# Gate and up projections of a SwiGLU layer: tokens as the stationary operand in six of nine chunks

## The chip, the core and the metric

The program runs on one core of a Trainium2 chip. TensorE (PE in the profile) multiplies matrices, VectorE (DVE) and ScalarE (ACT) work on the operands and results, GpSimd (POOL) and SyncE (SP) mainly issue transfers; 16 DMA engines move the data. The metric is the device time of one execution in microseconds (us). Three executions of the kernel before took 858.71, 859.27 and 859.91 us.

## The reference

One layer with three token mixers and a SwiGLU feed-forward part, for 512 tokens of 1024 channels. Only the feed-forward part is touched by the change:

```python
h2 = rms_norm(x, norm_ffn[l])
act = jax.nn.silu(jnp.einsum('bsd,df->bsf', h2, w_ffn_gate[l])) * jnp.einsum('bsd,df->bsf', h2, w_ffn_up[l])
x = x + jnp.einsum('bsf,fd->bsd', act, w_ffn_down[l])
```

The inner width is 2816. All of it is float32.

## The kernel before

**Precision.** Every float32 operand of a product is split into a high part (rounded by ScalarE with a copy) and a low part (VectorE subtracts the high part from the operand). A product is three matmuls: high by high, high by low, low by high. For a weight tile of 128 partitions by 1024 elements that is one copy on ScalarE (`split_a`, L1508, tiles `wh`) and one subtraction on VectorE (L1509, tiles `wl`). Both tiles come from a pool with three buffers each, so the split of the fourth product ahead starts when the oldest of three is used up.

**Seven products.** The inner width is cut into 11 chunks of 256 columns. Chunks 0 and 1 are computed directly (`direct_act`, with `ps_fg` and `ps_fu`). Chunks 2 to 10 are computed by a seven-product scheme for 2x2 blocks: the two halves of the 1024 input channels, the two halves of the tokens (256 each), and the two halves of the columns. The products go by the names in `ORDER`: 11, 12, S2, S1, S3, S4, 22. Four of them (S1 to S4) need sums of weight blocks, four need differences of token blocks (T1 to T4). The token blocks are prepared once (`prepare_b`): VectorE makes `hn` and the differences, ScalarE and VectorE split them into the `B0..h` and `B0..l` tiles.

**One chunk before** (`seven`, called for chunks 2 to 10). Four weight blocks (11, 21, 22, 12), each with gate and up, come by two transfers of 256 KB each (`load_a`, L1486, queue of SyncE), into the eight buffers of the pool `cor`; the load for a chunk is issued while the chunk before it is computed. VectorE makes the four sums of a chunk (`sums_a`, L1493). Each product is 24 matmuls (`product`, L315): the weights stand (128 x 128), and the 256 columns of half of the tokens move. A chunk's results lie in two PSUM tiles, `ps_y` and `ps_x`. Since S2, S3 and 22 add onto what lies in `ps_y`, ScalarE copies parts of it out in between (`tx` and `ty`, L1562): the matmuls of S3 may not begin before the copy behind S2 has been made. `finish_act` adds the last parts, applies Silu and multiplies.

**What sets the order.** A scheduler arranges each engine's instructions once, when the program is built; on the chip each engine works through its own list in order and stands still at an instruction whose operands are missing. The transfers wait in the lists of the engine that issues them (SP or POOL) in the same way. `make_a` is called three products ahead.

**Other weights in this kernel** are already used with tokens standing and 512 weight columns moving: the q, k and v projections (`tok_product`, L844, tiles `ps_q`). There some sums of blocks are made by transfers that add onto what lies in SBUF (`accum_op`, only issued by GpSimd), and the results are turned in 32 x 32 blocks by VectorE (L814).

Of the kernel before, what the change touches and what calls it, by code (L numbers as in the profile page):

```python
# [27 lines left out]
WARM = 9  # L28
GBUFS = 27
NDIRECT = 2  # L30
KD = 10
NTICK = (1, 1)
H = S // 2
# [29 lines left out]

@with_exitstack
def layer_kernel(ctx: ExitStack, tc: tile.TileContext, x, xt, vecs, w_in, w_qkv7, w_gate7, w_pool, w_rg, w_ig,
                 w_branch, w_br7, w_out, w_fg, w_fu, w_fd, w_fd7, out):
    nc = tc.nc
    act = nc.scalar.activation
    dve = nc.vector
# [21 lines left out]
    def cols(ap, k0, nk, c0, nc_):  # L91
        return ap[k0 * P:(k0 + nk) * P, c0:c0 + nc_].rearrange("(k p) c -> p k c", p=P)
# [878 lines left out]
    with ExitStack() as mix:  # L971
# [299 lines left out]
        def corner(shape, name, dt=F32):  # L1271

            return cor.tile([P] + shape, dt, tag="r", name=name)
# [91 lines left out]
    with ExitStack() as ffn:  # L1365
# [85 lines left out]
            dve.tensor_tensor(l, BN[key], h.bitcast(F32), ALU.subtract)  # L1451
            B[which, nm] = h, l

        def diff_b(nm, x, y):
            BN[nm] = corner([4, H], f"hn{nm}")
            dve.tensor_tensor(BN[nm], BN[x], BN[y], ALU.subtract)

        def prepare_b():
            nrm = [lambda k=k: norm2(k) for k in range(8)]
            return nrm[:4] + [lambda: split_b("11", (0, 0))] + nrm[4:] + [  # L1460
                lambda: split_b("21", (1, 0)),
                lambda: diff_b("T1", (0, 1), (0, 0)),
                lambda: diff_b("T2", (1, 1), "T1"),
                lambda: split_b("T2", "T2"),
                lambda: split_b("T1", "T1"),
                lambda: diff_b("T3", (1, 1), (0, 1)),
                lambda: split_b("T3", "T3"),
                lambda: split_b("22", (1, 1)),
                lambda: diff_b("T4", (1, 0), "T2"),
                lambda: split_b("T4", "T4")]  # L1470

        SUMS = {"S2": (("S3", "11", "21", ALU.subtract), ("S2", "22", "S3", ALU.subtract)),
                "S1": (("S1", "21", "22", ALU.add),),
                "S4": (("S4", "12", "S2", ALU.subtract),)}

        DOWN = NF // 2
        steps = [(c, nm) for c in range(NDIRECT, DOWN) for nm in ORDER]
        raw = {}
        A = {}
        made = [0, NDIRECT]  # L1480

        def load_a(c):
            for nm in ("11", "21", "22", "12"):
                raw[c, nm] = t = corner([2, 4, P], f"w{c}_{nm}")
                for w in range(2):
                    nc.sync.dma_start(t[:, w], cols((w_fg, w_fu)[w], KH[nm] * 4, 4, c * 256 + CH[nm] * P, P))  # L1486

        def sums_a(c, nm):
            for s_, x, y, op in SUMS.get(nm, ()):
                if (c, s_) in raw:  # L1490
                    continue
                raw[c, s_] = t = wp.tile([P, 2, 4, P], F32, tag="raw", name=f"w{c}_{s_}")
                dve.tensor_tensor(t, raw[c, x], raw[c, y], op)  # L1493

        def make_a(upto):
            while made[0] < min(upto, len(steps)):
                c, nm = steps[made[0]]
                made[0] += 1
                while made[1] < min(c + 2, DOWN):
                    load_a(made[1])  # L1500
                    made[1] += 1
                sums_a(c, nm)
                A[c, nm] = split_a(raw[c, nm], f"{c}_{nm}")

        def split_a(src, n):
            h, l = (t.rearrange("p (w k c) -> p w k c", w=2, k=4)
                    for t in weight_tiles("wh" + n, "wl" + n))
            act(h, src, AF.Copy)  # L1508
            dve.tensor_tensor(l, src, h.bitcast(F32), ALU.subtract)  # L1509
            return h, l  # L1510

        acts = []
        DB = {}


# [17 lines left out]
        def finish_act(t, ps, a):  # L1533

            v = two2(t)
            dve.tensor_tensor(v, v, in_order2(ps), ALU.add)
            act(t[:, 0, :], t[:, 0, :], AF.Silu)
            dve.tensor_tensor(a, t[:, 0, :], t[:, 1, :], ALU.mult)


        PRE = ("S2", "S1", "S3")
# [1 line left out]
        def seven(c):  # L1543
            a = g4([2, S], f"act{c}")
            tx, ty = g4([2, S], f"tx{c}"), g4([2, S], f"ty{c}")
            Y = fp.tile([P, 2, S], F32, tag="mm", name=f"ps_y{c}")
            X = fp.tile([P, 2, S], F32, tag="mm", name=f"ps_x{c}")
            lo, hi = slice(0, H), slice(H, S)
            plan = (("11", Y, 1, True, tx, lo, Y, hi),
                    ("12", X, 0, True, None, None, None, None),  # L1550
                    ("S2", Y, 1, False, tx, hi, Y, hi),
                    ("S1", X, 1, False, ty, hi, X, hi),
                    ("S3", Y, 1, False, ty, lo, Y, hi),
                    ("S4", X, 1, False, None, None, None, None),
                    ("22", Y, 0, False, None, None, None, None))
            n0 = steps.index((c, "11"))
            for n, (nm, ps, half, first, t, ts_, src, ss) in enumerate(plan):
                with tc.issue_after(last) if (c, n) == (NDIRECT, 3) else nullcontext():
                    make_a(n0 + n + 3)
                product(A.pop((c, nm)), B[0, WITH[nm]], ps, half, first, True)  # L1560
                if t is not None:
                    last = act(two2(t[:, :, ts_]), in_order2(src[:, :, ss]), AF.Copy).ins  # L1562
                if c == DOWN - 1 and nm in PRE:
                    split_d2("11", PRE.index(nm), 0, 0)
                if nm == "S4":
                    finish_act(tx, X, a[:, 0, :])
                if nm == "22":
                    finish_act(ty, Y, a[:, 1, :])
                if (c, n) in after:
                    after[c, n]()  # L1570
            acts.append(a)

        bg.extend([lambda: None, rms2] + prepare_b())
        for c in range(NDIRECT):
# [12 lines left out]

            if c < NDIRECT - 1:
                direct_act(0), direct_act(1)
            acts.append(a)  # L1590
        tick(len(bg))
        after = {(NDIRECT, 1): lambda: direct_act(0), (NDIRECT, 2): lambda: direct_act(1)}
# [164 lines left out]


_INS = ["x", "xt", "vecs", "w_in", "w_qkv7", "w_gate7", "w_pool", "w_rg", "w_ig", "w_branch", "w_br7", "w_out",
        "w_ffn_gate", "w_ffn_up", "w_ffn_down", "w_down7"]  # L1760


# [41 lines left out]
```

## Time and profile before

| what | value |
|---|---|
| median of three executions | 859.27 us |
| the profiled execution | 858.89 us |
| its span in the profile | 856.8 us |
| TensorE busy | 850.3 us (99%) |
| VectorE busy | 732.3 us (85%) |
| ScalarE busy | 533.3 us (62%) |
| GpSimd busy | 88.6 us (10%) |
| mean transfer rate | 180 GB/s |

In the profile a matmul's duration includes the time in which its results drain, while the next one already runs; the time that it takes away from the others is the distance from one start to the next. TensorE's clock was granted in full all through. Times inside the span are counted from its start. The gate and up products of chunks 2 to 10 lie at 580.50 to 749.46 us, behind the two direct chunks and ahead of the down projection.

### The profile page before, as it was taken

How to read it: one execution, taken by the hardware profiler on the slowest of the kernel's cores; microseconds unless marked ns; L12 is line 12 of the kernel's file. 1: busy time of each engine (PE TensorE's matmuls, PEld its weight loads, DVE VectorE, ACT ScalarE, POOL GpSimd, SP SyncE). 2: the span in 40 equal slices, each digit the busy share in tenths (PEclk: the TensorE clock that was granted, in tenths of full speed). 3: DMA queues.
4: the chain of work that ended last, by engine and by line, in shares of the span. 5: the costliest groups of instructions: out<-in, count | busy, mean ns of one | idle time of the engine just before them, and what ended most of it. 6: DMA issues, size and time to landing. Idle time of an engine off the chain costs nothing.

```text
span 856.8 us, 14307 instructions
## 1 busy us (share of the span) xinstructions
PE 850.3 (99%) x5483; PEld 781.2 (91%) x5483; DVE 732.3 (85%) x937; ACT 533.3 (62%) x863; POOL 88.6 (10%) x128
## 2 busy tenths in 40 slices
PE   9999999999999999999999999999999999999998
PEld 7888888888889988889889988889999999999998
DVE  7899898987897699967997877799988888999974
ACT  6554999658887657556665544455655555755642
POOL 1110002123324102000001100000000000121200
PEclk9999999999999999999999999999999999999999
DMA  9586356798585768846668854364533434797913
GB/s 343 160 286 205 101 167 200 215 316 262 141 257 129 228 170 239 246 116 171 174 204 212 182 197 148 99 164 136 145 99 109 114 101 142 221 238 204 199 32 123
DMA packets 141988, 154.09 MB, mean 180 GB/s; under 512 B 41696, under 2 KB 115424, under 8 KB 141920
## 3 DMA queue, kind: packets, MB, share of 16 engines
q1 hardware_dynamic: 129248, 107.30, 40.6%
q0 software_dynamic: 12528, 45.62, 22.5%
q8 instruction: 43, 0.70, 0.3%
q10 hardware_dynamic: 144, 0.26, 0.1%
q14 instruction: 25, 0.20, 0.1%
HBM read 132.71 MB, written 18.87 MB: 177 GB/s over the span
## 4 chain that ended last, share of the span: by engine, by line
PE 88%; ACT 4%; DVE 4%; issue 3%; POOL 1%; DMA 0%; DVEq 0%; POOLq 0%
PE ps_y L315 11%; PE ps_x L315 8%; PE ps_dy L1723 6%; PE ps_q L844 5%; PE ps_dx L1723 5%; PE ps_br L306 3%; PE ps_br L307 3%; PE ps_br L308 3%; PE ps_bY L1347 3%; PE ps_gy L315 3%; PE ps_gate L736 2%; PE ps_bX L1347 2%; PE ps_gx L315 2%; PE ps_pool L308 2%; PE ps_pool L306 2%
## 5 line engine op out<-in xcount | busy, mean ns | idle before, releaser
L141 ACT ACTIVATE whi<-raw 128x1024 fp32r<-128x1024 f32 x69 | 72.9, 1056 | 75.6 <-PE ps_br L307 18.4
L142 DVE TENSOR_TENSOR wlo<-raw,whi 128x1024 fp32r<-128x1024 f32 x69 | 84.2, 1220 | 22.4 <-ACT whi L141 21.9
L142 DVE TENSOR_TENSOR wlo<-qw,whi 128x1024 fp32r<-128x1024 f32 x48 | 58.3, 1220 | 11.6 <-ACT whi L141 11.2
L141 ACT ACTIVATE whi<-qw 128x1024 fp32r<-128x1024 f32 x48 | 50.4, 1052 | 23.6 <-PE ps_q L844 12.8
L1508 ACT ACTIVATE wh_S<-w_S 128x1024 fp32r<-128x1024 f32 x36 | 38.3, 1063 | 28.7 <-PE ps_y L315 20.0
L1629 POOL DMA_DIRECT2D dw<-in_w_down_dram x20 | 17.0, 855 | 305.3 <-DMA dw<-in_w_down_dram 247.7
L1509 DVE TENSOR_TENSOR wl_S<-w_S,wh_S 128x1024 fp32r<-128x1024 f32 x36 | 43.8, 1220 | 3.3 <-ACT wh_S L1508 3.3
L1508 ACT ACTIVATE wh<-w 128x1024 fp32r<-128x1024 f32 x27 | 28.6, 1061 | 28.0 <-PE ps_x L315 9.4
L1509 DVE TENSOR_TENSOR wl<-w,wh 128x1024 fp32r<-128x1024 f32 x27 | 32.9, 1220 | 8.2 <-ACT wh L1508 8.2
L1508 ACT ACTIVATE whdS<-dw 128x1024 fp32r<-128x1024 f32 x20 | 21.2, 1061 | 20.7 <-PE ps_dy L1723 10.6
L1155 DVE TENSOR_TENSOR_SCAN E<-K,ahead 128x512 f32<-128x512 f32 (+3 forms) x32 | 25.4, 814 | 4.6 <-ACT K L1151 4.6
L1509 DVE TENSOR_TENSOR wldS<-dw,whdS 128x1024 fp32r<-128x1024 f32 x20 | 24.3, 1221 | 5.2 <-ACT whdS L1508 5.2
L306 PE MATMUL ps_lru<-HH,whi 128*128 128x512 f32 x64 | 24.6, 384 | 0.0
L306 PE MATMUL ps_br<-yph,whi 128*128 128x512 f32 x64 | 24.4, 382 | 0.0
L306 PE MATMUL ps_gate<-HH,whi 128*128 128x512 f32 x64 | 24.4, 381 | 0.0
L307 PE MATMUL ps_br<-ypl,whi 128*128 128x512 f32 x64 | 24.3, 380 | 0.0
L306 PE MATMUL ps_pool<-HH,whi 128*128 128x512 f32 x64 | 24.3, 379 | 0.0
L306 PE MATMUL ps_br<-yHH,whi 128*128 128x512 f32 x64 | 24.3, 379 | 0.0
L307 PE MATMUL ps_lru<-HL,whi 128*128 128x512 f32 x64 | 24.3, 379 | 0.0
L308 PE MATMUL ps_lru<-HH,wlo 128*128 128x512 f32 x64 | 24.3, 379 | 0.0
L307 PE MATMUL ps_gate<-HL,whi 128*128 128x512 f32 x64 | 24.3, 379 | 0.0
L308 PE MATMUL ps_gate<-HH,wlo 128*128 128x512 f32 x64 | 24.3, 379 | 0.0
(742 smaller groups left out, 3432.1 us busy)
## 6 DMA issues: line engine op xcount, KB each, us to landing
raw<-in_w_in_dram SPq DMA_DIRECT2D x31, 512.0 KB, 5.1
qw<-in_w_qkv_dram SPq DMA_DIRECT2D x24, 512.0 KB, 7.2
dw<-in_w_down_dram POOLq DMA_DIRECT2D x20, 512.0 KB, 7.7
w<-in_w_ffn_gate_dram SPq DMA_DIRECT2D x36, 256.0 KB, 3.9
w<-in_w_ffn_up_dram SPq DMA_DIRECT2D x36, 256.0 KB, 4.1
raw<-in_w_branch_dram SPq DMA_DIRECT2D x16, 512.0 KB, 3.8
qw<-in_w_qkv_dram POOLq DMA_DIRECT2D x12, 512.0 KB, 7.6
g<-gd SPq DMA_DIRECT2D x24, 256.0 KB, 4.5
```

Source lines behind the costliest of these rows:

```text
L141: act(hi, raw, AF.Copy)
L142: los.append(dve.tensor_tensor(lo, raw, hi.bitcast(F32), ALU.subtract).ins)
L306: nc.tensor.matmul(ps, lh, rh, start=start, stop=False, skip_group_check=skip)
L307: nc.tensor.matmul(ps, lh, rl, start=False, stop=False, skip_group_check=skip)
L308: nc.tensor.matmul(ps, ll, rh, start=False, stop=stop, skip_group_check=skip)
L315: nc.tensor.matmul(o, a_[a][:, w, k, :], il2(b_[b][:, k, :]), start=first and n == k == 0, stop=last and n == 2 and k == 3, skip_group_che ...
L844: nc.tensor.matmul(ps[:, a, :], b_[:, k, ts_], il(a_[:, kk, :]), start=first and n == k == 0, stop=n == 2 and k == 3, skip_group_check=True)
L1155: dve.tensor_tensor_scan(E[:, c0:c0 + n][:, ::-1], K[:, c0 + 1:c0 + n + 1][:, ::-1], ahead[:, S - n:][:, ::-1], 0.0, ALU.mult, ALU.add)
L1347: nc.tensor.matmul(o, ah[x_][:, w, k, :], il2(b[k][y_]), start=first_ and n == k == 0, stop=n == 2 and k == 3, skip_group_check=True)
L1508: act(h, src, AF.Copy)
L1509: dve.tensor_tensor(l, src, h.bitcast(F32), ALU.subtract)
L1723: nc.tensor.matmul(o, a_[a][:, w, k0 + k, :], il2(b_[b][:, k, :]), start=first and i == k == 0, stop=last and i == 2 and k == nk - 1, skip ...
```

## The change

`NTOK = 3`. Chunks 2 to 7 become three units of two chunks (512 gate columns and 512 up columns each; `seven_tok`). In a unit the 2x2 blocks have gate against up as their column halves. Every product is now two pieces of 12 matmuls, in which a 128 x 128 block of tokens stands and 512 weight columns move. The results have the tokens on the partitions. ScalarE copies them out (`snap`), VectorE adds (`add`), ScalarE applies Silu, VectorE multiplies, turns the product in blocks of 32 x 32, and GpSimd stores it to a scratch tensor `ad` in DRAM; SyncE reads it back with the channels on the partitions (`load_act`), during the unit or chunk that follows. The order of the channels that this gives is answered by reordering the rows of the down weights on the host.

Chunks 8 to 10 keep weights standing and 256 token columns moving. What changes for them, too, is how the sums of weight blocks are made: with other signs of T1, T2 and T4 all sums become additions, and transfers issued by GpSimd make them (21+22; 11+21+22; then 21 onto 11, and 12 onto S2). In the units VectorE makes S2 (two additions a unit), transfers the others. The weights are laid out on the host so that every load is 512 KB of whole rows.

```diff
+NTOK = 3
...
-        def sums_a(c, nm):
-            for s_, x, y, op in SUMS.get(nm, ()):
...
-                dve.tensor_tensor(t, raw[c, x], raw[c, y], op)
...
+        def load_a(u):
+            if u >= NTOK:
+                for nm, more in (("11", ()), ("21", ("22",)), ("S2", ("21", "22"))):
+                    raw[u, nm, 0] = t = corner([2, 4, P], f"w{u}_{nm}")
+                    base = "11" if nm == "S2" else nm
+                    nc.sync.dma_start(t, lsrc(u, base))
+                    for m in more:
+                        nc.gpsimd.dma_start(t, lsrc(u, m), accum_op=ALU.add)
+                return
+            for nm in ("11", "21"):
+                for i in range(2):
+                    raw[u, nm, i] = t = corner([2, 512], f"w{u}_{nm}{i}")
+                    nc.sync.dma_start(t, usrc(u, nm, i))
+                    if nm == "21":
+                        nc.gpsimd.dma_start(t, usrc(u, "22", i), accum_op=ALU.add)
...
         def make_a(upto):
...
+                if u >= NTOK:
+                    for at, m in (("11", "12"), ("S1", "22")):
+                        if nm == at:
+                            raw[u, m, 0] = t = wp.tile([P, 2, 4, P], F32, tag="raw", name=f"w{u}_{m}")
+                            nc.sync.dma_start(t, lsrc(u, m))
+                    src = raw[u, FROM.get(nm, nm), 0]
+                    A[u, nm, i] = split_a(src, f"{u}_{nm}")
+                    for at, m in (("11", "21"), ("S2", "12")):
+                        if nm == at:
+                            nc.gpsimd.dma_start(src, lsrc(u, m), accum_op=ALU.add)
+                    continue
...
+                A[u, nm, i] = split_a(src, f"{u}_{nm}{i}", (2, 512))
+                if nm == "11":
+                    raw[u, "S2", i] = t = g4([2, 512], f"w{u}_S2{i}")
+                    dve.tensor_tensor(t, raw[u, "21", i], src, ALU.add)
+                    nc.gpsimd.dma_start(src, usrc(u, "21", i), accum_op=ALU.add)
+                elif nm == "S2":
+                    nc.gpsimd.dma_start(src, usrc(u, "12", i), accum_op=ALU.add)
...
+        def seven_tok(u):
...
+            def done(j):
+                g, t = v["g", j], v["u", j]
+                act(g, g, AF.Silu)
+                dve.scalar_tensor_tensor(t, t, -1.0, g, ALU.mult, ALU.mult)
+                dve.transpose(g.rearrange("p a c -> p (a c)"), t.rearrange("p a c -> p (a c)"))
+                for h in range(2):
+                    n = 4 * (2 * j + h)
+                    nc.gpsimd.dma_start(ad[u][:, n:n + 4].rearrange("m b (j i) -> (b j) m i", i=P),
+                                        g[:, h].rearrange("p (m i) -> p m i", i=P))
...
+                for i in range(2):
+                    make_a(n0 + 2 * n + i + 3)
+                    ah, al = A.pop((u, nm, i))
+                    for a in range(2):
+                        ts_ = slice(a * P, (a + 1) * P)
+                        for kk in range(2):
+                            k = 2 * i + kk
+                            for m, (b_, a_) in enumerate(((bh, ah), (bh, al), (bl, ah))):
+                                nc.tensor.matmul(ps[dst][:, a, :], b_[:, k, ts_], il(a_[:, kk, :]),
...
-        for c in range(NDIRECT, NF // 2):
-            if c == NF // 2 - 1:
+        for u in range(NTOK):
+            seven_tok(u)
+        for c in range(NDIRECT + 2 * NTOK, DOWN):
+            if c == DOWN - 1:
```

TensorE, the first matmuls of the gate and up products before. A row names the line, the operation, what is written, then what moves and what stands; `B011h` is the high part of token block 11, `wh2_11` the high part of chunk 2's weight block 11:

```order
L315 MATMUL ps_y2_5831<-B011h_5547,wh2_11_5811 128x256
L315 MATMUL ps_y2_5831<-B011l_5548,wh2_11_5811 128x256
L315 MATMUL ps_y2_5831<-B011h_5547,wl2_11_5812 128x256
L315 MATMUL ps_y2_5831<-B011h_5547,wh2_11_5811 128x256
L315 MATMUL ps_y2_5831<-B011l_5548,wh2_11_5811 128x256
```

The same place now; `wh0_110` is the high part of unit 0, block 11, piece 0, and `ps_yh0` the first result tile of the unit:

```order
L1665 MATMUL ps_yh0_5833<-wh0_110_5814,B011h_5550 128x512
L1665 MATMUL ps_yh0_5833<-wl0_110_5815,B011h_5550 128x512
L1665 MATMUL ps_yh0_5833<-wh0_110_5814,B011l_5551 128x512
L1665 MATMUL ps_yh0_5833<-wh0_110_5814,B011h_5550 128x512
L1665 MATMUL ps_yh0_5833<-wl0_110_5815,B011h_5550 128x512
```

What moves and what stands have changed places, and one matmul now does the columns of two.

VectorE at the start of the gate and up products before. `sg..` belong to the direct chunks, `w2_S3` and `w2_S2` are sums of chunk 2:

```order
L1509 TENSOR_TENSOR wl2_11_5812<-w2_11_5787,wh2_11_5811 128x1024
L1585 TENSOR_TENSOR sg00_5667<-sg00_5667,ps_fu_0_5577 128x512
L1585 TENSOR_TENSOR sg01_5672<-sg01_5672,ps_fu_0_5577 128x512
L1586 TENSOR_TENSOR act0_5666<-sg00_5667,rb2_5160 128x512
L1586 TENSOR_TENSOR act0_5666<-sg01_5672,rb2_5160 128x512
L1509 TENSOR_TENSOR wl2_12_5816<-w2_12_5796,wh2_12_5815 128x1024
L1493 TENSOR_TENSOR w2_S3_5819<-w2_11_5787,w2_21_5790 128x1024
L1583 TENSOR_TENSOR sg10_5888<-ps_fg_1_5677,rb2_5160 128x512
```

The same place now; `w0_210` is unit 0's block 21, piece 0, onto which a transfer has added block 22:

```order
L1550 TENSOR_TENSOR wl0_110_5815<-w0_110_5790,wh0_110_5814 128x1024
L1704 TENSOR_TENSOR sg00_5670<-sg00_5670,ps_fu_0_5580 128x512
L1704 TENSOR_TENSOR sg01_5675<-sg01_5675,ps_fu_0_5580 128x512
L1705 TENSOR_TENSOR act0_5669<-sg00_5670,rb2_5160 128x512
L1705 TENSOR_TENSOR act0_5669<-sg01_5675,rb2_5160 128x512
L1538 TENSOR_TENSOR w0_S20_5818<-w0_210_5794,w0_110_5790 128x1024
L1550 TENSOR_TENSOR wl0_111_5822<-w0_111_5792,wh0_111_5821 128x1024
L1538 TENSOR_TENSOR w0_S21_5825<-w0_211_5797,w0_111_5792 128x1024
L1702 TENSOR_TENSOR sg10_5900<-ps_fg_1_5680,rb2_5160 128x512
L1702 TENSOR_TENSOR sg11_5943<-ps_fg_1_5680,rb2_5160 128x512
L1550 TENSOR_TENSOR wl0_120_5829<-w0_120_5810,wh0_120_5828 128x1024
```

The two sums of S2, which need the transfers that add, stand ahead of the low parts of the second and third pieces (`wl0_111`, `wl0_120`).

ScalarE in the third of the chunks that keep their form (chunk 10, weights named `w5` now), from the split of S3 on; `tx10` is the copy out of PSUM behind S2. Before:

```order
L1508 ACTIVATE wh10_S3_7738<-w10_S3_7675 128x1024
L1508 ACTIVATE wh10_S4_7775<-w10_S4_7773 128x1024
L1562 ACTIVATE tx10_7671<-ps_y10_7673 128x2x256
L1508 ACTIVATE wh10_22_7810<-w10_22_7379 128x1024
L1562 ACTIVATE ty10_7672<-ps_x10_7674 128x2x256
```

Now:

```order
L1549 ACTIVATE wh5_S3_7188<-w5_11_6825 128x1024
L1549 ACTIVATE wh5_S4_7223<-w5_S2_6830 128x1024
L1603 ACTIVATE tx10_7124<-ps_y10_7126 128x2x256
L1549 ACTIVATE wh5_22_7258<-w5_22_7158 128x1024
L1603 ACTIVATE ty10_7125<-ps_x10_7127 128x2x256
```

The order is the same, but the split of S4 now reads `w5_S2`, onto which a transfer adds block 12 after the split of S2; before, VectorE had made that sum.

More of the change, by code (lines that the diff above doesn't have):

```diff
@@ L1510, in split_a @@
             return h, l
-        acts = []
+        acts = {}
         DB = {}
@@ L1555, in seven @@
                     ("22", Y, 0, False, None, None, None, None))
-            n0 = steps.index((c, "11"))
+            u = NTOK + c - (NDIRECT + 2 * NTOK)
+            n0 = steps.index((u, "11", 0))
             for n, (nm, ps, half, first, t, ts_, src, ss) in enumerate(plan):
-                with tc.issue_after(last) if (c, n) == (NDIRECT, 3) else nullcontext():
-                    make_a(n0 + n + 3)
-                product(A.pop((c, nm)), B[0, WITH[nm]], ps, half, first, True)
+                make_a(n0 + n + 3)
+                product(A.pop((u, nm, 0)), B[0, WITH[nm]], ps, half, first, True)
                 if t is not None:
@@ L1565, in seven @@
                 if nm == "S4":
-                    finish_act(tx, X, a[:, 0, :])
+                    finish_act(tx, X, a[:, 0, :], 1.0)
                 if nm == "22":
[L1568 to L1571, printed above, removed]
+                    finish_act(ty, Y, a[:, 1, :], -1.0)
+                if toload and nm in LOADS.get(u - NTOK, ()):
+                    with tc.issue_after(last):
+                        load_act()
@@ new lines, in seven, with load_act @@
+            acts[c] = a
+        ad = [dr.tile([4, S // 32, 4096], F32, tag=f"ad{u}", name=f"ad{u}") for u in range(NTOK)]
+        toload = []
+        LOADS = {0: ("S3",), 1: ("11",)}
+        def load_act():
+            c = toload.pop(0)
+            u, m = divmod(c - NDIRECT, 2)
+            acts[c] = t = g4([2, S], f"act{c}")
+            for w in range(2):
+                nc.sync.dma_start(t[:, w].rearrange("p (b i) -> p b i", i=32),
+                                  ad[u][2 * m + w].rearrange("b (p i) -> p b i", i=32))
```

122 lines of the change are left out of this document (89 added, 33 removed).

## The prediction

> **What bounds the kernel now.** I read the page's busy times first, then the windows of the stage, then the chain of waits through it.
>
> ```profile
> span 856.8 us, 14307 instructions
> PE 850.3 (99%) x5483; PEld 781.2 (91%) x5483; DVE 732.3 (85%) x937; ACT 533.3 (62%) x863; POOL 88.6 (10%) x128
> ```
>
> TensorE stands still for 6.5 us in all. The windows give each engine's busy time in the stage of chunks 2 to 7, then of chunks 8 to 10:
>
> ```profile
> 580.50:693.18 112.68, 112.68 (x1010) 112.64 (x1010) 103.22 (x97) 64.29 (x80) 0.00 (x0) 1.00 0.44 122
> 693.18:749.46 56.28, 56.28 (x506) 56.28 (x505) 50.03 (x49) 35.31 (x46) 2.57 (x3) 1.00 0.50 150
> ```
>
> The columns behind the length are PE, PEld, DVE, ACT, POOL, the clock, the DMA share and GB/s. TensorE never waits in either, and so a microsecond is worth a microsecond here. VectorE is at 92% of the first window, POOL does nothing, the transfers take under half. The chain names TensorE alone, with start, length and count:
>
> ```profile
> 580.50 2.68 PE ps_y L315 x24
> 583.17 2.68 PE ps_x L315 x24
> 585.85 2.70 PE ps_y L315 x24
> ...
> 728.02 5.36 PE ps_y L315 x48
> 733.38 2.68 PE ps_x L315 x24
> ...
> 741.42 2.68 PE ps_y L315 x24
> ```
>
> Each product of 24 matmuls of 256 columns takes 2.68 us, 111.7 ns each. The row of 48 holds the last product of one chunk and the first of the next, so chunk 10 begins at 730.70. A product in the new form (tokens standing, 512 weight columns moving) already runs in the q projections, where nothing makes it wait:
>
> ```profile
> 166.16 5.18 PE ps_q2S L844 x24
> ```
>
> That is 215.8 ns each, 107.9 for 256 columns.
>
> **The change part by part.** *Matmuls.* Six chunks have 42 products of 2.68 us, 112.6 us. Three units have 42 pieces of 12 matmuls, 42 x 5.18/2 = 108.8 us. Gain 3.8 us, all on the path. The bounds: nothing, if the spacing came out as before, and 3.9 with the 0.1 us that the first window has above 112.6.
> The Trainium skill (TensorE: Matmul & The Clock Gate, Back-to-back issue gap) gives N/2.4 GHz + 2.5 ns from start to start; that is 215.8 ns at 512 columns, as in the trace, but 109.2 at 256, where the trace has 111.7. By the page's formula the gain would be an estimated 1.3 us, not 3.8. The row measured in this very stage decides.
>
> *VectorE and ScalarE.* What the units issue, by these groups (count, busy us, mean ns):
>
> ```profile
> L1509 DVE TENSOR_TENSOR wl_S<-w_S,wh_S 128x1024 fp32r<-128x1024 f32 x36 | 43.8, 1220 | 3.3 <-ACT wh_S L1508 3.3
> L1493 DVE TENSOR_TENSOR w_S<-w,w 128x1024 f32<-128x1024 f32 x18 | 22.0, 1223 | 0.5
> L1493 DVE TENSOR_TENSOR w_S<-w,w_S 128x1024 f32<-128x1024 f32 x18 | 22.0, 1223 | 0.5
> L814 DVE STREAM_TRANSPOSE sq<-r 128x1024 f32<-128x1024 f32 x8 | 9.9, 1241 | 0.5 <-ACT r L823 0.5
> ```
>
> The 36 sums, four a chunk, go; a unit gets 14 low parts, 2 sums, 4 additions out of PSUM and 2 multiplications (I take 1.22 for each of the 22) and 2 turns of 1.24: 29.3 us of VectorE in 36.3 us, 81% against 92%. Followed step by step, an operand in a unit is ready at least 1.8 us before TensorE needs it, so I cost this at nothing. Its cover is TensorE's next two pieces, 5.2 us; if that were gone, the copies out of PSUM would delay the next product first. The 12 stores and 12 loads of turned results have a whole unit or chunk to land: nothing.
>
> *The start.* VectorE's two S2 sums of unit 0 wait for transfers that add 22 onto 21, and two low parts stand behind them. The load under the second sum goes into a buffer that before came free at 569.65; the groups are SP's issue, VectorE at that time, and landings of these loads:
>
> ```profile
> 569.65 0.37 SPq L1486 DMA_DIRECT2D w<-in_w_ffn_gate_dram  x1
> 578.70 1.22 DVE L1509 TENSOR_TENSOR wl<-w,wh 128x1024 fp32r<-128x1024 f32 x1
> L1486 SPq DMA_DIRECT2D w<-in_w_ffn_gate_dram x2: 368/612/857, 569.6 to 570.7; - x2
> DMA to landing us min/median/max: 4.1/4.9/5.2
> ```
>
> So POOL can issue the second addition at 574.55. What one takes is seen in other stages, behind loads and in a quieter place:
>
> ```profile
> L1282 POOL DMA_DIRECT2D bw<-in_w_br_dram x2: 848/870/892, 432.4 to 435.1; - x2
> DMA to landing us min/median/max: 8.6/8.6/8.6
> L270 POOL DMA_DIRECT2D bw<-in_w_br_dram x6: 835/844/852, 449.5 to 477.5; - x6
> DMA to landing us min/median/max: 5.1/5.6/8.8
> ```
>
> Nearest is the pair with loads beside it: 8.6, landing at 583.15. Then come the second sum (1.14 from start to start), two operations of direct chunk 1 (0.60 each) and the low part of the third piece (1.22): it is ready at 586.7. TensorE wants it two pieces after 580.50, at 585.7. Wait 1.1 us (with 5.1 none, with 8.8 1.3). The first sum, ready two microseconds earlier, is hidden by the first piece.
>
> *S4 in chunks 8 to 10.* Block 12 is added onto S2's buffer after S2's split. ScalarE's split of S4 stands ahead of the copy of `ps_y` behind S2, which S3 needs. In chunk 10 before (VectorE's split of S2, ScalarE's split of S4, the copy):
>
> ```profile
> 733.81 2.35 DVE L1509 TENSOR_TENSOR wl_S<-w_S,wh_S 128x1024 fp32r<-128x1024 f32 x2
> 738.72 1.07 ACT L1508 ACTIVATE wh_S<-w_S 128x1024 fp32r<-128x1024 f32 x1 [1.66 <-PE ps_y L315]
> 739.69 0.58 ACT L1562 ACTIVATE tx<-ps_y 128x512 f32<-128x512 f32 x1
> ```
>
> The copy ends at 740.27, S3 begins at 741.42: the split may be 1.15 us late, so the addition has to land by 739.87, 9.17 us into the chunk. The first split of the VectorE row ends at 735.0, 4.3 into the chunk, since the last addition and multiplication of chunk 9 and `al` lie ahead of it, then as now. Left over: 4.85 us. Chunk 9 begins 7 x 2.68 earlier, at 711.94; there the S2 split (the second row) ends 2.6 into the chunk, left over 6.5:
>
> ```profile
> 711.57 0.69 DVE L1538 TENSOR_TENSOR act<-tx 128x512 f32<-128x512 f32 x1
> 713.31 1.22 DVE L1509 TENSOR_TENSOR wl_S<-w_S,wh_S 128x1024 fp32r<-128x1024 f32 x1
> ```
>
> In chunk 8 the last multiplication and turn of unit 2 push the split to about 3.1, an estimate by the durations above; left over 6.0. Nearest for the additions are the first two of the down stage, at the same place in the program:
>
> ```profile
> L1629 POOL DMA_DIRECT2D dw<-in_w_down_dram x2: 849/853/857, 730.6 to 732.4; - x2
> DMA to landing us min/median/max: 5.4/5.9/6.5
> ```
>
> I take 5.9 for chunks 9 and 10, and 6.5 for chunk 8, which has two stores beside it. Waits: 0.5 + 0 + 1.1 = 1.6 us. The ends: at 5.1 it is 0.3 in chunk 10 alone, at 8.8 it is 2.8 + 2.3 + 4.0 = 9.1.
>
> *POOL's list* now has 33 additions and 12 stores ahead of or between those of the down stage. Where S2 of chunk 10 is built by two additions, the second waits for the first, and the S3 addition of chunk 9 stands behind both. It still lands some 3 us early by my walk through; likewise the one for chunk 10 behind `dw210`. Late next, if they slip: S3 of chunk 9. Cost nothing, bound 3 us.
>
> *Sum.* -3.8 + 1.1 + 1.6 = -1.1 us. From the profiled execution's 858.89 (2.1 beside its span) that is 857.8; the median of the runs lies 0.4 above that execution, so 858.2.
>
> **The rivals.** *The additions land early.* With the 5.1 to 5.6 of the quieter row everywhere nothing waits at the start nor in chunks 8 and 9, and 0.3 to 0.8 in chunk 10. For it: the DMA share of the stage is 0.44 to 0.50. Against: the start has a burst of loads. Time: -3.5 to -3.0, 855.8 to 856.3, say 856.0.
> The Trainium skill (DMA: Bandwidth & Descriptors, Anatomy of one DMA) fits a transfer issued by GpSimd as 2.0 us and its bytes at 436 GB/s, an estimated 3.2 us for 512 KB; by that nothing would wait at all and the sum would be 3.8 us less than before. No addition in this trace lands below 5.1.
>
> *The additions land late: slower.* One mechanism, the time L of one addition, decides at four places: the start (L - 7.5), chunk 8 (L - 6.0), chunk 9 (L - 6.5), chunk 10 (L - 4.85), each not below nothing. At the median of the down stage's 20,
>
> ```profile
> dw<-in_w_down_dram POOLq DMA_DIRECT2D x20, 512.0 KB, 7.7
> ```
>
> the waits are 0.2 + 1.7 + 1.2 + 2.85 = 5.95 us, 2.2 more than the gain: 861.4. From L = 7.1 on (start nothing, 3 x 7.1 - 17.35 = 3.9) it is slower than before. The landing times of 8.8 to 11.8 in a crowded part of that stage would make it worse; against it speaks that this crowd is of additions behind each other, here they are apart.
>
> *The spacing does not come down.* If TensorE gained nothing from the longer matmul, 2.7 us of waits would be added: 862. The q projections' row speaks against it; a half of the gain with my waits is 860.1, no difference.
>
> **How the numbers follow.** A measurement here tells 0.2% (1.7 us) from no change: faster means below 857.5, slower above 861.0. My case, waits of 2 to 4 us: chance 0.45, own range 857.0 to 859.8, a fifth of it faster. Early additions: 0.30, faster. Late additions: 0.17, slower. Half the spacing: 0.08, three parts no difference and one slower. Faster 0.09 + 0.30 = 0.39; no change 0.36 + 0.06 = 0.42; slower 0.19. The range from 855.4 (early additions, 0.4 to spare for the 0.1 us and the spread of the runs) to 861.8 (just past the late case's centre) leaves about 0.15 outside.
>
> **What would show it.** Right: rows of 12 or 24 matmuls with 512 columns spaced 216 ns in the units; TensorE's idle time small inside units 1 and 2; a wait of about 1 us for VectorE's third low part near 585; in chunk 10 a gap of about 1 us ahead of S3, with ScalarE's S4 split waiting for a transfer. VectorE at about 81% in the units. Wrong: gaps at unit ends or behind the copies out of PSUM, a wait for loads that SyncE issues behind `act` loads, or additions of over 8 us in chunks 8 to 10.

## The result, and the profile after

| | before | after |
|---|---|---|
| median of the executions | 859.48 us (858.71 to 859.91, 4) | 881.21 us (876.96 to 884.13, 4) |
| profiled execution / its span | 858.89 / 856.8 us | 880.38 / 878.6 us |

The ratio is 1.025, 95% interval 1.021 to 1.029: slower by 22 us, 19 us past the upper end of the predicted range. The page after, its span and its busy times:

```profile
span 878.6 us, 13277 instructions
PE 853.0 (97%) x4979; PEld 768.5 (87%) x4979; DVE 704.4 (80%) x907; ACT 530.6 (60%) x845; POOL 126.1 (14%) x173
```

TensorE now stands still for 25.6 us where it was 6.5. The windows of the units, then of chunks 8 to 10 (columns as before: length, PE, PEld, DVE, ACT, POOL, clock, DMA share, GB/s):

```profile
580.99:695.50 114.51, 111.19 (x507) 96.46 (x506) 85.26 (x76) 62.52 (x62) 26.47 (x32) 0.99 1.00 247
695.50:770.80 75.30, 60.87 (x504) 60.30 (x504) 41.81 (x41) 34.32 (x44) 12.27 (x16) 0.91 0.97 243
```

Before, these were 112.68 and 56.28 us with a DMA share of 0.44 and 0.50. Of the 21.8 us that the span grew, 20.9 lie here, 19.0 of them in three chunks whose matmuls did not change. The DMA engines are now busy nearly all through in both (shares of 1.00 and 0.97). The list of waits of TensorE shows where it stood:

```profile
PE ps_y L316 <- ACT tx L1603: 14.4, 3, 9.4
PE ps_xl L1665 <- DVE wl L1550: 2.2, 1, 2.2
PE ps_yh L1665 <- DVE wl L1550: 1.1, 1, 1.1
```

The first row is three stops of 14.4 us in all, the longest 9.4: S3 of chunks 8, 9 and 10, which waits for the copy `tx`. The other two are the start. The chain of waits (start, length, what; a DMA from its issue to its landing):

```profile
574.98 11.52 DMA w<-in_w_ffn_dram
590.13 6.92 PE ps_xl L1665 x23
679.93 5.18 PE ps_yh L1665 x24
698.85 15.04 DMA w_S<-in_w_ffnl_dram
714.96 0.59 ACT tx L1603
715.59 5.31 PE ps_y L316 x24
738.51 2.94 PE ps_y L316 x24
751.66 7.68 DMA w_S<-in_w_ffnl_dram
761.04 4.57 PE ps_y L316 x24
```

The products in the units take 5.18 us as forecast. The DMA rows are additions, the one in chunk 8 with 15 us. And behind three of the stops the same 24 matmuls take longer than without a stop: 6.92 for 5.18, 5.31 and 4.57 for 2.68, 6.3 us in all. (Behind the short stop in chunk 9 it is 2.94, at the full clock.) The windows of 2 us say why; behind the length stand PE, PEld, DVE, ACT, POOL, and then the clock:

```profile
592.00:594.00 2.00, 2.00 (x6) 1.55 (x6) 2.00 (x4) 0.48 (x1) 0.00 (x0) 0.50 1.05 223
718.00:720.00 2.00, 2.00 (x11) 2.00 (x11) 0.00 (x0) 0.00 (x0) 0.00 (x0) 0.50 1.04 203
722.00:724.00 2.00, 2.00 (x21) 2.00 (x20) 1.52 (x2) 0.86 (x2) 0.56 (x1) 1.00 1.08 168
```

TensorE is busy all through in each. But in the second window, at half the clock, it has 11 matmuls of 256 columns in hand, in the third, at the full clock, 21; of these it begins 9 and 18, the others still drain from the window before. ScalarE's rows of chunk 8 (what ended its idle time stands in brackets) show that S4 was not the only late block:

```profile
707.44 1.06 ACT L1549 ACTIVATE wh_S<-w 128x1024 fp32r<-128x1024 f32 x1 [7.83 <-DMA w<-in_w_ffnl_dram]
714.00 1.06 ACT L1549 ACTIVATE wh_S<-w_S 128x1024 fp32r<-128x1024 f32 x1 [5.50 <-DMA w_S<-in_w_ffnl_dram]
```

The first row is S3's block; TensorE had reached S3 at 706.2. The account of the stage: -3.8 for the matmuls, +17.7 in stops, +6.3 at the lower clock, 0.7 not assigned, 20.9.

### The profile page after: what moved, and what is told of

It reads as the page before. It is cut to its first block, busy times and chain, and to the rows that moved or that the text cites. A ratio compares the mean times of both kernels' runs of the same rounds, so it can differ in the third digit from the quotient of the medians.

```text
span 878.6 us, 13277 instructions
## 1 busy us (share of the span) xinstructions
PE 853.0 (97%) x4979; PEld 768.5 (87%) x4979; DVE 704.4 (80%) x907; ACT 530.6 (60%) x845; POOL 126.1 (14%) x173
## 4 chain that ended last, share of the span: by engine, by line
PE 71%; issue 9%; DVE 7%; DMA 6%; ACT 5%; POOL 2%; SPq 0%; ACTq 0%; POOLq 0%; DVEq 0%
PE ps_dy L1844 6%; PE ps_q L845 5%; PE ps_dx L1844 5%; PE ps_yh L1665 5%; PE ps_xh L1665 4%; PE ps_y L316 3%; PE ps_br L308 3%; PE ps_br L309 3%; PE ps_br L307 3%; DMA w_S<-in_w_ffnl_dram 3%; PE ps_bY L1348 2%; PE ps_gy L316 2%; DVE wlo L143 2%; PE ps_xl L1665 2%; PE ps_bX L1348 2%
## 5 line engine op out<-in xcount | busy, mean ns | idle before, releaser
L1550 DVE TENSOR_TENSOR wl_S<-w_S,wh_S 128x1024 fp32r<-128x1024 f32 x18 | 22.0, 1223 | 24.6 <-ACT wh_S L1549 24.6
L1550 DVE TENSOR_TENSOR wl_S<-w,wh_S 128x1024 fp32r<-128x1024 f32 x18 | 22.0, 1223 | 22.2 <-ACT wh_S L1549 22.2
L1549 ACT ACTIVATE wh_S<-w_S 128x1024 fp32r<-128x1024 f32 x18 | 19.0, 1053 | 21.6 <-DMA w_S<-in_w_ffnl_dram 10.0
L1549 ACT ACTIVATE wh_S<-w 128x1024 fp32r<-128x1024 f32 x18 | 19.0, 1057 | 20.6 <-DMA w<-in_w_ffnl_dram 9.7
L308 PE MATMUL ps_br<-yHL,whi 128*128 128x512 f32 x64 | 24.4, 381 | 0.1
```

The lines of the kernel that those rows point to most:

```text
L308: nc.tensor.matmul(ps, lh, rl, start=False, stop=False, skip_group_check=skip)
```

## The experiments

Times are medians, the ratio is to the kernel before on the same chip.

**VectorE's sums in chunks 8 to 10.**

```diff
-                for nm, more in (("11", ()), ("21", ("22",)), ("S2", ("21", "22"))):
+                for nm in ("11", "21", "22", "12"):
                     raw[u, nm, 0] = t = corner([2, 4, P], f"w{u}_{nm}")
+                    nc.sync.dma_start(t, lsrc(u, nm))
...
+                        dve.tensor_tensor(t, raw[u, x, 0], raw[u, y, 0], ALU.add)
```

> The kernel after, but in chunks 8 to 10 VectorE makes the four sums again from four plainly loaded blocks; the 15 additions by transfer of these chunks are gone, the units stay as they are. Theory (the S3 and S4 additions of these chunks land late and hold ScalarE and TensorE; the stops then cost clock as well): the stops of 9.4, about 1.7 and about 3.5 us and the slower matmuls behind them (2.6 and 1.9 us) go, 19 us less than after, about 861 to 862; the three chunks take 56.3 us as before. Rival 1 (the loads of act in pieces of 128 bytes crowd the queue of SyncE and the DMA engines, whatever makes the sums): the plainly loaded blocks come late as well, 868 or more, with waits for transfers in chunks 8 to 10. Rival 2 (VectorE had no room there): slower than 862 with waits for VectorE.

859.02 us, ratio 1.000 (0.999 to 1.001): 22 us less than after, 2 to 3 more than the theory asked for. The three chunks take 56.27 us without a stop:

```profile
693.38:749.65 56.27, 56.27 (x505) 56.27 (x505) 53.25 (x52) 34.50 (x45) 5.68 (x7) 1.00 0.73 205
```

The units, with all their additions, stores and loads, cost nothing beyond the start; VectorE has room at 95% (53.25 of 56.27).

**The start, too.**

```diff
+                    if nm == "21" and u == 0:
+                        t2 = wp.tile([P, 2, 512], F32, tag="raw", name=f"w{u}_e22{i}")
+                        nc.sync.dma_start(t2, usrc(u, "22", i))
+                        dve.tensor_tensor(t, t, t2, ALU.add)
```

> As the run before this one, and in unit 0 VectorE also adds block 22 onto block 21 from a plain load (1 MB more loaded, two VectorE operations of about 1.2 us). Theory (the start loses 3.4 us to two late additions and 1.8 us to the clock behind these stops): 5 us less than with the chunks' sums alone, about 856 to 857, which is a little faster than before the change. Rival (the loads at the start are late by themselves, because the transfers of the whole stage are crowded there): no or under 2 us less, 859 or more.

857.18 us, ratio 0.9969 (0.9958 to 0.998): this version is faster than both kernels. One stop of 0.4 us is left in the stage, and its two windows add up to 165.55 us where before had 168.96:

```profile
580.25:689.52 109.27, 108.88 (x506) 95.34 (x506) 86.53 (x79) 62.21 (x62) 19.08 (x24) 1.00 0.90 227
689.52:745.80 56.28, 56.28 (x505) 56.28 (x505) 53.27 (x52) 34.49 (x45) 5.79 (x8) 1.00 0.73 203
```

That is the matmuls' 3.8 us less the one stop: the first term of the prediction, seen alone. The medians of the two versions differ by 1.8 us where 5 were expected. In the trace of the other version the start has the stops of after (2.2 and 1.0 us), but the clock stays at 1.00, so in that execution the 1.8 us of clock were not there to gain (four of its ten executions have a mean clock of 0.998, and they are the four longest); of the other 3.2 us the profiled spans show 3.5, the medians less, and this version's profiled execution, 855.29 us, is its shortest.

**S4 alone by VectorE.**

```diff
+                    if nm == "S4":
+                        dve.tensor_tensor(raw[u, "S2", 0], raw[u, "S2", 0], raw[u, "12", 0], ALU.add)
...
-                    for at, m in (("11", "21"), ("S2", "12")):
+                    for at, m in (("11", "21"),):
```

> The kernel after, but in chunks 8 to 10 VectorE adds block 12 onto S2's buffer (from the plain load of 12 that is there for the product 12 anyway), so the S4 additions by transfer are gone, and nothing else: four additions a chunk are left, S3's among them. Theory (S4's addition is the longest of several late ones): S3's block in chunk 8 stays 3 us late, the stops of chunks 9 and 10 shrink to under 2 us, 864 to 870. Rival (the prediction's step alone, late S4 additions, is the whole loss): all stops of chunks 8 to 10 go, 860 to 863, as with all sums by VectorE.

872.61 us, ratio 1.016 (1.014 to 1.017): 8.6 us less than after, smaller than either side said. The additions of S4 are gone, and `ps_y` waits for `tx` all the same, 7.0 us in two stops: now for S3's addition, which lands 9.9 us behind its issue in chunk 9. So it is not S4 alone. That addition was also issued late. On GpSimd's list it stands behind the second addition to S2 of chunk 10, which waits for the landing of the first (the chain, POOL being the issues):

```profile
711.75 0.91 POOL w_S L1498
...
718.99 0.57 POOL w_S L1498
719.56 9.89 DMA w<-in_w_ffnl_dram
```

Chunk 9 begins at 716.33 here, so the issue is 3.2 us into the chunk; in the kernel after it was 2.7 us ahead of it. This is the slip that the prediction called "late next".

**The copy ahead of the split.**

```diff
+                    with tc.issue_after(cp[0]) if nm == "S4" else nullcontext():
+                        A[u, nm, i] = split_a(src, f"{u}_{nm}")
```

> The kernel after with one order changed: in chunks 8 to 10 ScalarE's split of S4 stands behind the copy tx that S3 waits for, not ahead of it. All additions stay. Theory (the DMA engines are full there and every added block comes late, S3's as well as S4's): in chunk 8 S3's own block is split only at about 708.5, 3 us late, and S4's block, landed at 713.9, comes 2 us later than S4 could begin, so most of the stop only moves from S3 to S4: 3 to 8 us less than after, 872 to 878. Rival (the place of the split ahead of the copy is the cause, as the prediction priced it): the stops of chunks 8 to 10 go, 862 to 866.

877.3 us, ratio 1.021 (1.020 to 1.023): 3.9 us less than after. The stops moved, from S3 to the product behind it:

```profile
PE ps_x L316 <- ACT ty L1605: 7.1, 2, 5.1
PE ps_y L316 <- ACT tx L1605: 2.9, 1, 2.9
```

The place of ScalarE's split adds a little; the late blocks are the loss.

**S2 by VectorE: three of ten transfers fewer, S3 and S4 untouched.**

```diff
-                for nm, more in (("11", ()), ("21", ("22",)), ("S2", ("21", "22"))):
+                for nm, more in (("11", ()), ("21", ("22",))):
...
+                    if nm == "11":
+                        raw[u, "S2", 0] = t = g4([2, 4, P], f"w{u}_S2")
+                        dve.tensor_tensor(t, raw[u, "21", 0], src, ALU.add)
```

> The kernel after, but in chunks 8 to 10 VectorE makes S2 from the buffers of 21 (with 22 added) and 11, as in the units; the load and the two additions that made S2 are gone, three of ten transfers of 512 KB a chunk. S3's and S4's additions stay by transfer, at the same places. Theory (how late S4's addition lands depends on how much else the DMA engines and GpSimd's queue carry there): they land in 7 to 9 us instead of 15.0, 7.7 and 7.7, stops of 3 to 8 us in all, 865 to 873. Rival (S4's addition is late for its own place, whatever else is carried): 877 or more, the chain still names over 12 us for it in chunk 8.

864.77 us, ratio 1.008 (1.006 to 1.009): 16.4 us less than after, though the additions that TensorE waits for kept their places. They land in 5.4 to 10.7 us, 7.0 at the median (after: 6.6 to 15.0, 8.0), and the stops for `tx` are 4.3 us. What is late depends on what else is under way. But this also took a wait out of GpSimd's list, where the second addition to S2 stands behind the landing of the first; two runs look at the two apart.

**The same transfers, another order on GpSimd.**

```diff
+                        if u == NTOK:
+                            nc.gpsimd.dma_start(t, lsrc(u, m), accum_op=ALU.add)
+                        else:
+                            later.append((t, lsrc(u, m)))
...
+                            with tc.issue_after(s4.ins):
+                                nc.gpsimd.dma_start(*later.pop(0), accum_op=ALU.add)
```

> The kernel after with all its transfers, but in another order on GpSimd's list: the additions that build 21+22 and S2 of chunks 9 and 10 stand behind the S4 addition of the chunk before, not ahead of its S3 addition. Theory A (the loss comes from GpSimd's list: an addition that waits for the one before it on the same buffer holds S3's and S4's additions behind it): S3's addition of chunk 8 is issued several us earlier, the stops of chunks 8 to 10 shrink to 2 to 6 us, 862 to 868, about what leaving S2's additions out gave (864.8). Theory B (the number of bytes on the DMA engines): the additions land as late as before, 874 to 882; the stops may move to later chunks. Between, 868 to 874, both have a part.

879.87 us, ratio 1.023 (1.022 to 1.025): no gain that the intervals can tell. Five stops instead of three, 16.8 us instead of 14.4, and in other places: 1.5 us where chunk 8 had 9.4, but 10.3 in chunk 10. There the additions for S3 and S4 stand on the list behind a transfer of the down projection that starts at 747.84, 9.6 us into the chunk:

```profile
747.84 0.84 POOL L1758 DMA_DIRECT2D dw<-in_w_down_dram  x1 [10.27 <-DVE Bd110l L1579]
748.38 1.17 POOL L1532 DMA_DIRECT2D w<-in_w_ffnl_dram  x1
748.91 1.51 POOL L1532 DMA_DIRECT2D w_S<-in_w_ffnl_dram  x1
```

So this order takes a loss away at one end of the list and makes one at the other. It doesn't show that the list has no part.

**Two loads back.**

```diff
+                for n in range(2):
+                    nc.sync.dma_start(corner([2, 4, P], f"wx{u}_{n}"), lsrc(u, ("11", "21")[n]))
```

> VectorE makes S2 of chunks 8 to 10 (864.8 before), and SyncE loads two blocks of 512 KB a chunk more into buffers that nobody reads, in the place of the load and the two additions that were left out. Theory B (bytes): most of the loss comes back, 872 to 880. Theory A (GpSimd's list): the two loads hold nobody on GpSimd, 864 to 868.

870.67 us, ratio 1.013 (1.011 to 1.016): 5.9 us come back with two plain loads of 512 KB a chunk that nobody reads and nobody on GpSimd waits for. The additions for S3 and S4 land later with them. The landing times without the two loads, then with them:

```profile
DMA to landing us min/median/max: 5.4/7.0/10.7
```

```profile
DMA to landing us min/median/max: 7.8/8.5/11.2
```

The time is a little under the 872 of the theory of bytes and outside its rival's 864 to 868. So more transfers alone make the additions late. Of the other 10.5 us it stays open how much is the higher price of an addition (measured in the next run) and how much the wait in the list.

**Chunk additions without units.** Chunks 2 to 7 as in the first run, chunks 8 to 10 as after, no stores and loads of `act`.

```diff
-NTOK = 3
+NTOK = 0
+ADD0 = 6
...
+            if u < ADD0:
+                for nm in ("11", "21", "22", "12"):
```

> No units: all nine chunks have weights standing and 256 columns moving; chunks 2 to 7 get their sums from VectorE, chunks 8 to 10 from additions by transfer exactly as after. No stores and loads of act. Theory (the additions land late since the transfers of the units, the stores and the loads of act are still going on): in the quiet stage ahead they land in 5 to 8 us as the prediction took them, the waits are 1 to 6 us, 860 to 866. Rival (ten transfers of 512 KB in 18.8 us a chunk are too many by themselves): 870 or more, with stops of over 5 us for additions in chunks 8 to 10.

869.97 us, ratio 1.012 (1.010 to 1.014), between the two: stops of 7.9 us, the longest 4.1, in a stage that was quiet ahead. So ten transfers a chunk cost 11 us by themselves; with the units ahead of them the same additions cost 22 (859.0 to 881.2). Its queues in a quiet stretch (590 to 650: 13 plain loads) and in the crowded one (690 to 755: additions on q0) tell the price of each (packets, MB, share of 16 engines):

```profile
q1 hardware_dynamic: 1872, 6.82, 33.7%
...
q0 software_dynamic: 1630, 5.96, 53.5%
q1 hardware_dynamic: 2314, 7.46, 31.0%
```

33.7% of 60 us over 13 loads is 1.55 us of all 16 engines for one of 512 KB; 53.5% of 65 us for 5.96 MB is 3.06 us for an addition of 512 KB, twice as much. The last row, of the plain loads beside these additions, gives 1.42 us for 512 KB, so it is not the crowd that makes the difference. An estimate from the first two rows, of the engines' time that a chunk of 18.76 us asks for (the loads of `act` and of the down weights left out), beside the measured length of the three chunks (from the first matmul of chunk 8 to the first of the down projection):

| version | loads + additions a chunk | engines' time a chunk (estimate) | chunks 8 to 10 |
|---|---|---|---|
| sums by VectorE | 4 + 0 | 6.2 us | 56.3 us |
| S2 by VectorE | 4 + 3 | 15.4 us | 62.9 us |
| two loads back | 6 + 3 | 18.5 us | 68.8 us |
| S4 by VectorE | 5 + 4 | 20.0 us | 66.5 us |
| after | 5 + 5 | 23.1 us | 75.5 us |

After asks for more than the chunk lasts. The only pair out of order is the version without S4's addition, which takes away a transfer that TensorE waits for. The table goes with the crowd, but the versions differ in GpSimd's list as well.

**Long pieces.** The turned results are stored and read back in pieces of 2 KB, in another order, so the channels of `act` come out of order.

```diff
-                nc.sync.dma_start(t[:, w].rearrange("p (b i) -> p b i", i=32),
-                                  ad[u][2 * m + w].rearrange("b (p i) -> p b i", i=32))
+                nc.sync.dma_start(t[:, w], ad[u][2 * m + w].rearrange("b (q c) -> (b q) c", c=512))
```

> The kernel after with all its additions, but the turned results are stored and read back in pieces of 2 KB instead of 512 and 128 bytes (the same bytes, in another order, so the channels of act come out of order). Theory A (the small pieces fill the DMA engines and delay the additions): the additions in chunks 8 to 10 land in 6 to 8 us, the stops there shrink from 14.6 to 3 to 6 us, the clock stays, 864 to 869 in all. Theory B (the additions themselves, 33 of 512 KB through the software queue, are too many and stand behind each other): 877 to 882, the chain still names the addition of chunk 8 with over 12 us.

873.83 us, ratio 1.018 (1.015 to 1.021): 7.4 us less than after, between the theories. The loads of `act`, after and then here (SyncE's issue in ns min/median/max, and the landing):

```profile
L1624 SPq DMA_DIRECT2D act<-ad x12: 377/2370/7862, 638.9 to 727.3; - x12
DMA to landing us min/median/max: 5.4/9.9/15.1
```

```profile
L1624 SPq DMA_DIRECT2D act<-ad x12: 382/432/1190, 638.4 to 723.2; - x12
DMA to landing us min/median/max: 6.0/6.9/11.4
```

Issuing one load in pieces of 128 bytes holds SyncE's queue 2.4 us at the median and up to 7.9. The small pieces have a part, but 9.7 us of stops for `tx` stay without them.

**The crowd without anyone waiting.** To the version with VectorE's sums in chunks 8 to 10, five additions a chunk onto spare rows in DRAM were added.

```diff
+                    if nm in MORE:
+                        nc.gpsimd.dma_start(spare[nm], lsrc(u, MORE[nm]), accum_op=ALU.add)
```

> The kernel with VectorE's sums in chunks 8 to 10, and in each of these chunks five additions of 512 KB issued by GpSimd at the same five places as after, but onto spare rows in DRAM that nobody reads (and five plain stores of 512 KB from weights to these rows during unit 1). The bytes and the crowd are there, no operand hangs on an addition. Theory (the loss needs both, a crowded DMA and an operand asked for 6 us before its use): the plain blocks are loaded a chunk ahead and have the slack, 859 to 862. Rival (the crowd alone delays every load in these chunks): 868 or more.

895.68 us, ratio 1.043 (1.041 to 1.044), and inconclusive: nothing held the spare additions where they were written, and the scheduler put them at the program's beginning,

```profile
L1526 POOL DMA_DIRECT2D spS<-in_w_ffnl_dram x9: 802/1121/1431, 50.4 to 98.8; - x9
```

where TensorE was busy for 79.0 of the first 100 us (before: 98.5). It says nothing on chunks 8 to 10, and was not repeated.

**A stop in the quiet kernel.**

```diff
+                if (c, nm) == (5, "S3"):
+                    for _ in range(12):
+                        act(raw[c, nm], raw[c, nm], AF.Copy)
```

> The kernel before with one stop put in: ahead of the split of S3 in chunk 5 ScalarE copies the block onto itself twelve times (12.7 us of work, the values stay the same), so TensorE stands still some 8 to 10 us once. Theory (a stop of this length makes the granted clock fall, and the matmuls behind it run slower): the time grows by the stop and 2 to 3 us more, with the clock under 0.9 in the 10 us behind it and 24 matmuls of 256 columns taking over 4 us instead of 2.68. Rival (the lower clock after came from the 512-column matmuls or from the transfers): the time grows by the stop alone, the clock stays at 1.00.

862.51 us, ratio 1.004 (1.003 to 1.005). ScalarE took most of the copies in its idle time: TensorE stopped for 1.8 us in two pieces, and the clock of the profiled execution stayed at 1.00 (three of the five have 0.998). Too short to decide; so with 26 copies:

> The kernel before with 26 copies of S3's block of chunk 5 onto itself instead of 12, so 15 us more of ScalarE's work and a real stop of TensorE of over 8 us, in a stage with quiet transfers and 256-column matmuls alone. Theory (a stop of more than about 3 us makes the granted clock fall to 0.5 for some 4 us behind it): the windows show 0.5 behind the stop, the first 24 matmuls take over 4 us. Rival (the clock fell after because of crowded transfers): the clock is 1.00 behind the stop.

879.63 us in the one run; the stop is 16.5 us. Windows at its beginning, behind it, and 4 us later:

```profile
650.00:652.00 2.00, 0.00 (x0) 0.00 (x0) 0.00 (x0) 2.00 (x3) 0.00 (x0) 0.75 0.00 0
668.00:670.00 2.00, 2.00 (x11) 2.00 (x11) 2.00 (x3) 0.00 (x0) 0.00 (x0) 0.50 0.06 16
672.00:674.00 2.00, 2.00 (x21) 2.00 (x20) 1.23 (x1) 0.95 (x3) 0.00 (x0) 1.00 0.86 250
```

With the DMA engines at rest (share 0.00) and 256-column matmuls alone, the clock falls in the stop and comes back some 6 us behind it. So a long stop alone lowered the clock in this run; it took neither transfers nor the longer matmul.

**Four units.** The faster version with `NTOK = 4`, so only chunk 10 has 256 columns moving.

```diff
-NTOK = 3
+NTOK = 4
-        LOADS = {0: ("S3",), 1: ("11",)}
+        LOADS = {0: ("S2", "S3")}
```

> The version with VectorE's sums in the remaining chunks and at the start, with four units instead of three (chunks 2 to 9), so only chunk 10 has 256 columns moving. Theory (each unit saves 14 products of 2.68 us against 14 pieces of 2.59, 1.26 us): 1.3 us less than with three units, 855.5 to 856.5, with no stop in the units. Rival (the results of the fourth unit are read back during chunk 10 in pieces of 128 bytes, beside the down weights, and come late): 859 or more, with waits at the beginning of the down projection.

863.16 us, ratio 1.005 (1.003 to 1.006): the rival. The chain leads through the store and the load of the fourth unit's results into the down projection,

```profile
735.01 7.86 DMA ad<-v3g
...
743.00 3.30 DMA act<-ad
```

and TensorE stops for 4.2 us in chunk 10 and 2.4 in the down projection. Three units leave the results a chunk or more to land, four don't.

## Why the prediction was wrong, step by step

**Matmuls: right.** -3.8 us forecast; 5.18 us for each 24 matmuls in the chain, and -3.4 with one stop of 0.4 in the faster version. The half spacing and no spacing rivals fall.

**VectorE in the units: right.** No stop inside or between units; the first window has it at 85.26 of 114.51 us, 74% (81% forecast, for units without stops).

**The start: right place, wrong size.** The third low part was waited for, 2.2 us. The second was, too, 1.1 us: the prediction had the first sum hidden by the first piece, but the first addition took 9.4 us. 1.1 us was forecast from a landing time of 8.6; the second addition took 11.5, the stops were 3.3 us, 1.7 more went at the lower clock.

**S4 in chunks 8 to 10: this step failed, by its size.** The mechanism (addition, ScalarE's split, the copy behind it, S3) is what the chain shows. The landing times taken, 5.9 to 6.5 us, came from a quieter place; measured are 15.0, 7.7 and 7.7. With these and the start's 11.5, the allowances of the prediction (7.5, 6.0, 6.5, 4.85) give 4.0 + 9.0 + 1.2 + 2.85 = 17.1 us of stops; 17.7 came. The upper end of 8.8 for L was no bound, since the change itself fills the engines; the text had seen landings of up to 11.8 in a crowd and set them aside. What came is its rival "the additions land late", given 0.17, with landing times beyond those it reckoned with.

**Why the landing times were mis-sized: the transfers were costed one by one.** The stores and loads of the turned results, costed at nothing, do land in time. But the sum of all transfers was never formed. The page of before had the rows for it (packets, MB, share of 16 engines over 856.8 us):

```profile
q1 hardware_dynamic: 129248, 107.30, 40.6%
q0 software_dynamic: 12528, 45.62, 22.5%
```

3.24 and 4.23 us of all engines per MB, so 1.70 us for a load and 2.22 for a transfer of GpSimd's queue of 512 KB; five of each is an estimated 19.6 us in a chunk of 18.76. The DMA share of 0.44 to 0.50 that spoke for early additions was that of four loads' bytes a chunk. That more transfers lengthen the landing is shown (7.0 to 8.5 us at the median with two plain loads a chunk); that this sum is the whole of the loss is argued from the table.

**GpSimd's list "nothing", "late next: S3 of chunk 9": not settled.** In the kernel after, the S4 additions that TensorE waited for were issued when S2's split was done, so there the list cost nothing that the chain shows. S3's block was late in chunk 8 and in time in chunks 9 and 10. But once S4's additions were gone, S3 of chunk 9 was held by the list, as the prediction had it, with a stop of 4.9 us and not under the bound of 3.

**Left out: the clock.** 6.3 us that no step had. In the trace of before TensorE never stops for long in this stage, so it shows no such fall.

The Trainium skill (TensorE: Matmul & The Clock Gate, What's actually happening) says that the clock is halved after an idle window of about 3.4 us and given back after a busy one of about that length, and that the window runs free. The stops of 16.5, 9.4 and 3.5 us agree for the fall; the full clock came back 6.3, 5.0 and 4.0 us behind them, later than that. The window that runs free may be why the start, with stops of 1.1 and 2.2 us, lost the clock in one trace (0.50 at 592 to 594) and not in another with nearly the same stops (with two loads back and stops of 1.0 and 2.2 us it was lost again); no run here shows the window itself.

The rule of the DMA: Bandwidth & Descriptors page of the Trainium skill (Anatomy of one DMA) that the prediction weighed, an estimated 3.2 us for 512 KB, was nowhere near: in chunks 8 to 10 the S3 and S4 additions landed in 6.6 to 15.0 us.

## What to carry to other kernels

Before sums move from an engine to accumulating transfers, add up the DMA time of all transfers in the stage against its length. The queue rows of the profile give us per MB, and a landing time read in a quiet stage is no guide once the sum comes near the stage's length. Look, too, at what stands ahead of each addition on the list that issues it. Use additions where the operand is asked for long ahead, as in the units here, and keep VectorE's sums where it is asked for two or three products ahead. Price a stop of TensorE of several us as the stop and some 2 us more for the lower clock behind it.

## What the runs showed of the hardware

- An addition of 512 KB by transfer took 3.06 us of all 16 DMA engines in the crowded chunks, a plain load 1.42 beside them and 1.55 in a quiet stretch.
- Loads in pieces of 128 bytes held SyncE's queue for 2.4 us at the median and up to 7.9 us each, against 0.43 in pieces of 2 KB.
- In the run with one long stop TensorE's clock fell to 0.50 within it, and came back some 6 us behind it.
